# Start addresses of the large SBUF tiles in a four-layer transformer kernel on one core

## Chip, core and metric

The kernel runs on one core of one Trainium2 chip. The metric is the device time of one execution in microseconds (us). Three runs of the kernel before gave 1937.42, 1938.02 and 1940.01 us; their median is 1938.02 us.

## What is computed

The input is one sequence of 512 tokens with 1024 features. It goes through two blocks of two layers each; all weights and activations are float32. The parts that the change touches are these:

```python
# block 1, layer 0: RG-LRU mixer; layer 1: stick-breaking attention; each followed by a SwiGLU
def _rglru_mixer(h, ...):
    proj = h @ w_in                               # gate_br, x_br
    xc = causal depthwise conv of x_br, 4 taps, plus conv_b
    r, i = sigmoid(xc @ w_r + b_r), sigmoid(xc @ w_i + b_i)   # 4 blocks of 256 x 256
    a = exp(8 * r * log_sigmoid(lam)); u = sqrt(1 - a*a) * (i * xc)
    hs = linear scan over time of (a, u)
    return (hs * gelu(gate_br)) @ w_out
def _stick_breaking_attention(q, k, v):           # 16 heads of 64
    z = q k^T / 8
    w[t] = sigmoid(z[t]) * product of sigmoid(-z[s]) over the keys s between t and the query
    return w @ v
# block 2, even layer: global, windowed and memory attention; odd layer: neighbourhood and memory attention
```

Everything else is matrix products with RMS norms, softmax and gates around them.

## The kernel before, in words

**Layout of the work.** Features lie on the 128 partitions, the 512 tokens along the free axis, so that an activation of 1024 features is eight tiles of [128, 512]. A float32 value is split into two parts of the type float32r, a high part `h` and the rest `l`, and a product is three matmuls (`mm3`, lines 161 to 163): high weight times high activation, high weight times low activation, low weight times high activation. The first operand of a matmul is the stationary one (128 columns of a weight tile), the second the moving one (256 or 512 columns of an activation tile).

```python
def mm3(self, out, wh, wl, xh, xl, start, stop):
    mm = self.nc.tensor.matmul
    mm(out, wh, xh, start=start, stop=False)      # L161
    mm(out, wh, xl, start=False, stop=False)      # L162
    mm(out, wl, xh, start=False, stop=stop)       # L163
```

`proj` runs `mm3` over the k-tiles of one output tile, 24 matmuls for 1024 inputs, into one PSUM bank. In `v_proj` (lines 569 to 571) the roles are exchanged: a 128-token piece of an activation tile is stationary and a weight tile moves, the bank changes after every third matmul. The same `mm3` also multiplies two activation tiles: the scores and values of the memory attention. The scores of the global attention are lines 1085 and 1086, its values lines 1118 and 1119; there too both operands are activation tiles. Matmuls that turn a [128, 128] piece (lines 684, 957, 1108, 1186, 1432) have a piece of an `f` tile as the stationary operand and the identity as the moving one.

**Buffers.** All tiles come from one pool with one buffer each; they are laid one behind the other in the order in which they are asked for, each rounded up to 32 bytes per partition. Rings (`Slots`) hand them out oldest-freed first:

| tiles | bytes in a partition | used for | start in the partition, multiples of 2048 taken off |
|---|---|---|---|
| s0-s47, k0-k3 | 32 each | factors per partition | - |
| r0-r59 (float32r) | 2048 each | activations, keys, queries, values, split | 1792 |
| f0-f25 (float32, 516 columns) | 2064, laid 2080 apart | everything not split, residual | all different, multiples of 32 |
| w32 x3, wh x6, wl x6 | 2048 each | weights as loaded, high part, low part | 576 |
| par, ones, mhalf, ebase, lamc, warm, ident, identb, sbmask, fgain, pair | small | constants | - |

The first tile of the pool lies at byte 16512, so r0 is at 18176, wh_0 at 201280 and wl_0 at 213568. A weight tile holds four k-tiles of 128 columns; their stationary operands start 512 bytes apart, at 576, 1088, 1600 and 64 (multiples of 2048 taken off), against 1792 of a moving activation tile.

**Order of the work.** `fetch` (line 134 on) takes the weights in the order of a plan, 512 columns at a time: SP's queue loads a `w` tile, ScalarE writes `wh` (line 142), VectorE writes `wl` (line 143). Up to six chunks are ready ahead. The order on TensorE is the order of tracing: in the attention layers the projections of the next heads are traced between the scores and the values of the present ones, so that TensorE works while VectorE and ScalarE do the softmax.

**Places that the change touches.** In `rglru` the projection is multiplied by the norm into columns 3 to 514 of an `f` tile (line 398), after GpSimd has cleared columns 0 to 2 (line 397); GpSimd starts the convolution (line 401) and three VectorE instructions add the other taps over all 512 columns (line 403), eight times. In `sb_score` (lines 649 to 654) each head's running product is an exclusive scan: GpSimd writes 1.0 into a column, VectorE scans w keys into the w columns behind it, and w of the w + 1 columns are used; 64 times. `warm` (line 105 on) clears its own [128, 512] bfloat16 tile and runs 11 matmuls on it before the first weights are there.

Of the kernel before, what the change touches and what calls it, by code (L numbers as in the profile page):

```python
# [29 lines left out]
FW = 516  # L30


class Slots:
    """Fixed buffers handed out oldest-freed first; the order of tracing gives the waits."""
# [30 lines left out]
class Net:  # L65
    def __init__(self, ctx, tc, nc, a):
# [6 lines left out]
        self.keep = Slots([cp.tile([128, 8], F32, name=f"k{i}") for i in range(4)])  # L73
        self.R = Slots([cp.tile([128, 512], F32R, name=f"r{i}") for i in range(N_R)])
        self.F = Slots([cp.tile([128, FW], F32, name=f"f{i}") for i in range(N_F)])
        self.P = Slots([pp.tile([128, 512], F32, name=f"p{i}") for i in range(8)])
# [3 lines left out]
        self.plan, self.fetched, self.ready = [], 0, deque()  # L80
        self.taken, self.pinned = 0, set()
        par = cp.tile([128, N_PARAM], F32, name="par")
        nc.sync.dma_start(par, a["params"])
        self.par = par
        ones = cp.tile([128, 1], F32, name="ones")
        nc.vector.memset(ones, 1.0)
        self.ones = ones
        mhalf = cp.tile([128, 8], F32, name="mhalf")
        nc.scalar.activation(mhalf, ones.to_broadcast([128, 8]), AF.Copy, scale=-0.5)
        self.mhalf = mhalf  # L90
        ebase = cp.tile([128, 8], F32, name="ebase")
        nc.vector.memset(ebase, 2.718281828459045)
        self.ebase = ebase
        self.scr = cp.tile([128, 32], F32, name="lamc")

    def const(self, name, n):
        t = self.cp.tile([128, n], F32, name=name)
        self.nc.sync.dma_start(t, self.a["c_" + name])
        return t

    def warm(self, n=10):
        """Keeps the tensor engine busy while the first tiles are loaded."""
        nc = self.nc
        z = self.cp.tile([128, 512], BF16, name="warm")
        nc.vector.memset(z, 0.0)
        ps = self.P.get()
        for _ in range(n):
            nc.tensor.matmul(ps, z[:, 0:128], z, start=True, stop=True)
        self.P.put(ps)

# [4 lines left out]
    def small(self, n, keep=False):  # L115
        """Scratch for per-partition scalars; a ring, so short-lived unless `keep`."""
        ring = self.keep if keep else self.sm
        t = ring.get()
        ring.put(t)
        return t[:, 0:n]  # L120
# [6 lines left out]
    def chunks(self, key, width):  # L127
        """Adds the array slice `key` (name, indices...) to the plan, CH columns at a time."""
        for c0 in range(0, width, CH):
            self.plan.append((key, c0, min(width, c0 + CH)))  # L130
# [18 lines left out]
    def weights(self, key, c0=0):  # L149
        """The plan's next chunk as two float32r parts whose sum is the weight."""  # L150
        pinned = min(self.pinned, default=len(self.plan))
        while self.fetched < min(len(self.plan), pinned + N_W) and len(self.ready) <= AHEAD:
            self.fetch()
        self.taken = self.fetched - len(self.ready)
        k, c, h, l = self.ready.popleft()
        assert (k, c) == (key, c0), ((k, c), (key, c0))
        return h, l
# [7 lines left out]
    def open(self, key, kt, off=0, out=None, n=512):  # L165
        """A product over kt k-tiles, run in one or more pieces."""
# [20 lines left out]
    def proj(self, key, XH, XL, off=0, out=None, n=512):  # L187
        """key: [128, K] of weights, k-tile by k-tile; returns a PSUM tile [128, n]."""
        return self.advance(self.open(key, len(XH), off, out, n), XH, XL)

    def split(self, src, eng="v"):
        """float32 [128, 512] in SBUF -> two float32r tiles."""
# [34 lines left out]
    def rstd(self, src, cols, width=D, keep=False):  # L227
        """src: [128, n] sums of squares laid by token -> 1/sqrt(mean + eps)."""
# [12 lines left out]
    def spread(self, r, cols):  # L241
        """r [128 tokens, blocks] -> tile [128, 128 * blocks] with r along the free axis."""
# [12 lines left out]
    def norm_end(self, st, acc, shifted=False):  # L255
        """Factors by token for blocks 0, 128, 256, 384 and, half a block on, 64, 192, 320."""
# [8 lines left out]
    def tok(self, st):  # L265
        """1/rms by token, on partitions."""
# [4 lines left out]
    def row(self, st):  # L271
        """1/rms of every token on every partition."""
# [5 lines left out]
    def residual_norm(self, ms, gain, late=False, shifted=False):  # L278
        """ms: callables that finish residual tile k; splits x * gain and gathers the norm."""
# [25 lines left out]
    def start_out(self, outs, name, kt, YH, YL, tiles=2, last=None):  # L305
        """Runs the first output tiles, kept in `outs`, over the k-tiles at hand (the last one up to `last`)."""
# [32 lines left out]
    def lam_consts(self):  # L339
        """c/2 with c = 8 log_sigmoid(lam), and -c/2."""  # L340
# [43 lines left out]
    def rglru(self, st, gain_next):  # L384
# [5 lines left out]
        for kind, n in self.RG_STEPS:  # L390
            if kind == "x":
                xcs, ch, cl = [], [], []
                for mt in range(2):
                    m = 2 * n + mt
                    ps = self.proj(("w_rg", 8 + m), st["XH"], st["XL"])
                    xbt, xb = self.f(515)
                    pool.memset(xb[:, 0:3], 0.0)
                    v.tensor_tensor(xb[:, 3:515], ps, self.row(st), op=ALU.mult)
                    self.P.put(ps)
                    xct, xc = self.f()  # L400
                    pool.tensor_scalar(xc, xb[:, 3:515], self.p("conv_w", 24 + m), self.p("conv_b", m), op0=ALU.mult, op1=ALU.add)
                    for j in (2, 1, 0):
                        v.scalar_tensor_tensor(xc, xb[:, j : j + 512], self.p("conv_w", 8 * j + m), xc, op0=ALU.mult, op1=ALU.add)
# [70 lines left out]
    def silu_part(self, ps, R):  # L474
        """PSUM gate -> tile A with silu(gate) = A / 2."""
# [40 lines left out]
    def stack_q(self, q32):  # L516
        """[head A; head B] float32 -> [hA; lA] and [hB; lB], each [128, 512] float32r."""
# [11 lines left out]
    def stack_k(self, k32):  # L529
        """[head A; head B] float32 -> per head ([h; h], [l; l]) float32r."""  # L530
# [14 lines left out]
    def v_evac(self, ps, r, out):  # L545
        """PSUM [128 tokens, heads * 64] times r -> out [128, heads * 128] laid [h l] per head."""
# [7 lines left out]
    def v_proj(self, keys, lhs, n):  # L554
        """keys: per k-tile (key, column) of weights [128, n]; lhs(k, t): (h, l) [128, 128] of
        activations for token tile t. Returns a PSUM tile per token tile."""
# [18 lines left out]
    def fold_heads(self, oA, oB):  # L575
        """Two heads' PSUM [from h; from l] -> float32 tile [A; B] of the sums."""
# [10 lines left out]
    def evac_split(self, ps, n):  # L587
        """PSUM [:, :n] -> (h, l) float32r tiles."""
# [37 lines left out]
    def sb_score(self, QK, A, parts):  # L626
        """parts: (head, q-block, column) sharing one bank; keys run backwards from the diagonal."""
# [21 lines left out]
        for idx, (hd, i, o) in enumerate(parts):  # L649
            w = 128 * (i + 1)  # L650
            c = o + idx
            nc.gpsimd.memset(it[:, c : c + 1], 1.0)
            nc.vector.tensor_tensor_scan(it[:, c + 1 : c + 1 + w], a[:, o : o + w], self.zeros[:, :w], 1.0, op0=ALU.mult, op1=ALU.add)  # L653
            nc.vector.tensor_tensor(wt[:, o : o + w], b[:, o : o + w][:, ::-1], it[:, c : c + w][:, ::-1], op=ALU.mult)
# [13 lines left out]
    def sb_values(self, W, V, between):  # L668
        """Weights [query, key] and values -> the pair's output, split."""
# [4 lines left out]
        def turn(*blocks):  # L674
            """blocks: (head, query blocks, key block), one after the other."""
# [54 lines left out]
    def sb_mixer(self, st, gain_next):  # L730
        nc, cp = self.nc, self.cp
        self.identb = cp.tile([128, 128], BF16, name="identb")
# [3 lines left out]
        self.sbmask = cp.tile([128, 256], BF16, name="sbmask")  # L736
# [57 lines left out]
    def double_norm(self, ms):  # L794
        """x <- rmsnorm(x, final_g), and the split of x * final_g * gain2[0] for the next layer."""
        nc = self.nc
        fg = self.p("final_g", 0, 8)
        gain = self.cp.tile([128, 8], F32, name="fgain")
# [40 lines left out]
    def mem_kv(self, layer):  # L839
        """Keys [dim, 256] of two heads per tile and values [token, 512], all split."""  # L840
# [139 lines left out]
    def gated(self, yt, A):  # L980
        """(A / 2) * y, split."""
# [35 lines left out]
    def rope(self, ps, R, g, gs):  # L1017
        """Rotated q * g (before its own rms) and a callable for the rms factors [128 tokens, 2 * block + head]."""
# [80 lines left out]
    def gqa_value(self, W, V):  # L1099
        """Turn and product steps; V[j]: [128 keys, 128] = [h | l] of the head's values."""  # L1100
# [40 lines left out]
    def win_score(self, Q, K, hd):  # L1141
        """hd: head number; softmax with sink over the keys WIN[b] of query block b."""
# [60 lines left out]
    def pair_values(self, value, W, V, between, after=None):  # L1203
        """Both heads of a pair; `between` is issued while the turned weights are split, `after` while the result is."""
# [15 lines left out]
    def even_mixer(self, st, gain_next):  # L1220
# [10 lines left out]
        self.pairsel = self.const("pair", 2)  # L1231
# [144 lines left out]
    def grid_bias(self):  # L1376
        """rpb_c as bias[head][query (col, row) of 16 columns][key (col, row) of 32 columns]."""
# [9 lines left out]
    def na_score(self, Q, K, hd):  # L1387
# [15 lines left out]
        # (query block, first key, keys, bias, place)  # L1403
# [173 lines left out]
    def final(self, name, YH, YL, outs):  # L1577
        """Residual and last norm; the last two tiles run half by half so that the first half's output overlaps."""
# [45 lines left out]
    def run(self, stop=None):  # L1624
# [9 lines left out]
        self.ident = self.const("ident", 128)  # L1634
# [21 lines left out]
def _cols(w, m0=0, m1=None):  # L1656
    """[K, M] -> [M/128, 128, K]: per 128 columns, the k-tiles side by side."""
# [5 lines left out]
def _rows(w):  # L1663
    """[K, n] -> [128, K/128 * n]: the k-tiles side by side."""
# [8 lines left out]
def _arrays(i):  # L1673
# [30 lines left out]
    g4 = np.stack([i["a_w_r"][0], i["a_w_i"][0]], 1)  # [4, 2, 256, 256]  # L1704
# [73 lines left out]
def _grid_order():  # L1778
    """Token number (row-major on the grid) at each place of the column-major order."""
# [33 lines left out]
```

## Time and profile before

| | |
|---|---|
| median of three runs | 1938.02 us (1937.42 to 1940.01) |
| span of the profiled execution, first to last instruction | 1936.2 us; its time as a run is not listed apart, so the span stands 1.8 us below the median |
| TensorE busy (matmuls / weight loads) | 1893.0 us, 98% / 1546.1 us, 80% |
| VectorE, ScalarE, GpSimd busy | 62%, 46%, 17% |
| DMA | 204 MB, 37% of 16 engines |
| granted TensorE clock, mean over the span | 0.997 of 2.4 GHz |

How to read it: a matmul's record runs from its start to the modelled end of its output, some 0.39 us, and the next one starts long before that; records overlap. So TensorE's busy time says only where it had no gap, and what a matmul costs is the distance from its start to the next one's start. The timeline shows starts to 0.01 us; a distance is taken over many matmuls.

### The profile page before, as it was taken

How to read it: one execution, taken by the hardware profiler on the slowest of the kernel's cores; microseconds unless marked ns; L12 is line 12 of the kernel's file. 1: busy time of each engine (PE TensorE's matmuls, PEld its weight loads, DVE VectorE, ACT ScalarE, POOL GpSimd, SP SyncE). 2: the span in 40 equal slices, each digit the busy share in tenths (PEclk: the TensorE clock that was granted, in tenths of full speed). 3: DMA queues.
4: the chain of work that ended last, by engine and by line, in shares of the span. 5: the costliest groups of instructions: out<-in, count | busy, mean ns of one | idle time of the engine just before them, and what ended most of it. 6: DMA issues, size and time to landing. Idle time of an engine off the chain costs nothing. (4 is left out here: it accounts for less than half of the span.)

```text
span 1936.2 us, 25837 instructions
## 1 busy us (share of the span) xinstructions
PE 1893.0 (98%) x9003; PEld 1546.1 (80%) x9003; DVE 1208.5 (62%) x2181; ACT 881.8 (46%) x1701; POOL 330.9 (17%) x386
## 2 busy tenths in 40 slices
PE   8999999999999999999999999999999999999998
PEld 5778888888888777788888888888878888888877
DVE  8886555553336888555555336679897665776753
ACT  4764333333335565433333335456565444455542
POOL 5442000000001211200000121222212421322310
PEclk9999999999999999999999999999999999999999
DMA  4333333333334443333333334322433432554532
GB/s 137 113 106 104 92 96 95 93 93 94 95 96 134 135 124 99 93 92 93 94 95 103 101 109 132 98 77 60 111 106 96 120 104 87 141 146 137 141 99 73
DMA packets 124803, 204.04 MB, mean 105 GB/s; under 512 B 21209, under 2 KB 31193, under 8 KB 124673
## 3 DMA queue, kind: packets, MB, share of 16 engines
q1 hardware_dynamic: 124672, 202.39, 37.4%
q8 instruction: 71, 1.16, 0.3%
q14 instruction: 60, 0.48, 0.1%
HBM read 168.76 MB, written 4.40 MB: 89 GB/s over the span
## 5 line engine op out<-in xcount | busy, mean ns | idle before, releaser
L162 PE MATMUL p<-r,wh 128*128 128x512 f32 (+1 forms) x2216 | 864.5, 390 | 7.1 <-DVE r L223 5.5
L163 PE MATMUL p<-r,wl 128*128 128x512 f32 (+1 forms) x2216 | 864.5, 390 | 6.5 <-DVE wl L143 6.4
L161 PE MATMUL p<-r,wh 128*128 128x512 f32 (+1 forms) x2216 | 868.0, 392 | 0.1
L142 ACT CAST wh<-w 128x512 fp32r<-128x512 f32 x608 | 371.1, 615 | 677.4 <-PE p L162 499.8
L143 DVE TENSOR_TENSOR wl<-w,wh 128x512 fp32r<-128x512 f32 x608 | 443.0, 732 | 352.2 <-ACT wh L142 345.5
L163 PEld LDWEIGHTS p<-r,wl 128*128 128x128 f32 x2216 | 416.8, 188 | 104.2 <-DVE wl L143 9.6
L162 PEld LDWEIGHTS p<-r,wh 128*128 128x128 f32 x2216 | 417.2, 188 | 102.7 <-DVE r L223 7.6
L161 PEld LDWEIGHTS p<-r,wh 128*128 128x128 f32 x2216 | 416.8, 188 | 94.6 <-ACT wh L142 1.7
L198 POOL TENSOR_TENSOR r<-f,r 128x512 fp32r<-128x512 f32 x102 | 141.6, 1390 | 471.5 <-ACT r L196 451.9
L196 ACT CAST r<-f 128x512 fp32r<-128x512 f32 x146 | 90.7, 621 | 176.4 <-DVE f L504 65.5
L214 POOL TENSOR_TENSOR f<-f,f 128x512 f32<-128x512 f32 x40 | 55.4, 1391 | 492.9 <-ACT f L208 492.9
L478 DVE TENSOR_TENSOR f<-p,f 128x512 f32<-128x512 f32 x68 | 47.0, 691 | 89.8 <-PE p L163 89.0
L593 DVE TENSOR_TENSOR r<-p,r 128x512 fp32r<-128x512 f32 (+2 forms) x152 | 90.6, 640 | 4.1 <-ACT r L592 3.6
L592 ACT CAST r<-p 128x512 fp32r<-128x512 f32 (+2 forms) x152 | 77.3, 558 | 12.2 <-PE p L1108 5.7
L569 PE MATMUL p<-wh,r 128*128 128x512 f32 (+1 forms) x192 | 72.1, 375 | 1.0 <-DVE f L582 1.0
L502 DVE TENSOR_TENSOR f<-p,f 128x512 f32<-128x512 f32 x44 | 30.4, 692 | 67.1 <-PE p L163 67.1
L571 PE MATMUL p<-wh,r 128*128 128x512 f32 (+1 forms) x192 | 71.8, 374 | 0.0
L570 PE MATMUL p<-wl,r 128*128 128x512 f32 (+1 forms) x192 | 71.8, 374 | 0.0
L481 ACT ACTIVATE f<-f 128x512 f32<-128x512 f32 x68 | 43.1, 633 | 39.8 <-DVE f L478 39.8
L653 DVE TENSOR_TENSOR_SCAN f<-f,f 128x128 f32<-128x128 f32 (+3 forms) x64 | 51.0, 828 | 14.1 <-ACT f L645 14.1
L921 DVE TENSOR_SCALAR f<-f,s 128x256 f32<-128x256 f32 (+3 forms) x160 | 56.6, 418 | 1.1
L482 DVE SCALAR_TENSOR_TENSOR f<-f,f 128x512 f32<-128x512 f32 x68 | 47.3, 696 | 12.1 <-ACT f L481 7.9
(216 smaller groups left out, 1812.1 us busy)
## 6 DMA issues: line engine op xcount, KB each, us to landing
w<-w_gu SPq DMA_DIRECT2D x176, 256.0 KB, 3.0
r<-r SPq DMA_DIRECT2D x240, 128.0 KB, 2.5
w<-w_d SPq DMA_DIRECT2D x80, 256.0 KB, 2.7
w<-wo_m SPq DMA_DIRECT2D x64, 256.0 KB, 2.9
w<-we_m SPq DMA_DIRECT2D x52, 256.0 KB, 3.0
w<-w_rg SPq DMA_DIRECT2D x32, 256.0 KB, 2.9
w<-w_sqk SPq DMA_DIRECT2D x32, 256.0 KB, 2.9
w<-we_o SPq DMA_DIRECT2D x24, 256.0 KB, 2.6
```

The lines of the kernel that those rows point to most:

```text
L142: nc.scalar.copy(h[:, :n], w[:, :n])
L143: nc.vector.tensor_tensor(l[:, :n], w[:, :n], h[:, :n].bitcast(F32), op=ALU.subtract)
L161: mm(out, wh, xh, start=start, stop=False)
L162: mm(out, wh, xl, start=False, stop=False)
L163: mm(out, wl, xh, start=False, stop=stop)
L196: nc.scalar.copy(h, src)
L198: e.tensor_tensor(l, src, h.bitcast(F32), op=ALU.subtract)
L569: mm(o, xh, h[:, s], start=st, stop=False)
L570: mm(o, xh, l[:, s], start=False, stop=False)
L571: mm(o, xl, h[:, s], start=False, stop=sp)
L592: nc.scalar.copy(h[:, :n], ps[:, :n])
L593: nc.vector.tensor_tensor(l[:, :n], ps[:, :n], h[:, :n].bitcast(F32), op=ALU.subtract)
```

## The change

The large tiles (r, f, w32, wh, wl) become 2048 bytes each and are asked for behind all small ones; a pad of 28 columns (128 bytes as laid) puts the first of them, r0, at byte 20480, ten times 2048. From there each follows the last, so that every large tile starts at a multiple of 2048 (r0 20480, f0 143360, w32_0 196608, wh_0 202752, wl_0 215040). Their numbers stay the same. What lay in the way goes: f tiles have 512 columns instead of 516, the convolution and the scan get along without extra columns, and `warm` borrows an f tile. The rest of the diff takes comments and docstrings out.

```diff
+SMALL_PAD = 28
-FW = 516
+FW = 512
...
         self.keep = Slots([cp.tile([128, 8], F32, name=f"k{i}") for i in range(4)])
+        self.P = Slots([pp.tile([128, 512], F32, name=f"p{i}") for i in range(8)])
...
+        par = cp.tile([128, N_PARAM], F32, name="par")
+        ones = cp.tile([128, 1], F32, name="ones")
...
+        self.ident = cp.tile([128, 128], F32, name="ident")
+        self.identb = cp.tile([128, 128], BF16, name="identb")
+        self.sbmask = cp.tile([128, 256], BF16, name="sbmask")
+        self.fgain = cp.tile([128, 8], F32, name="fgain")
+        self.pairsel = cp.tile([128, 2], F32, name="pair")
+
+        cp.tile([128, SMALL_PAD], F32, name="pad")
         self.R = Slots([cp.tile([128, 512], F32R, name=f"r{i}") for i in range(N_R)])
         self.F = Slots([cp.tile([128, FW], F32, name=f"f{i}") for i in range(N_F)])
...
-        z = self.cp.tile([128, 512], BF16, name="warm")
-        nc.vector.memset(z, 0.0)
+        t, f = self.f(256)
+        z = f.bitcast(BF16)
+        nc.vector.memset(f, 0.0)
         ps = self.P.get()
         for _ in range(n):
             nc.tensor.matmul(ps, z[:, 0:128], z, start=True, stop=True)
         self.P.put(ps)
+        self.F.put(t)
...
-                    xbt, xb = self.f(515)
-                    pool.memset(xb[:, 0:3], 0.0)
-                    v.tensor_tensor(xb[:, 3:515], ps, self.row(st), op=ALU.mult)
+                    xbt, xb = self.f()
+                    v.tensor_tensor(xb, ps, self.row(st), op=ALU.mult)
...
-                    pool.tensor_scalar(xc, xb[:, 3:515], self.p("conv_w", 24 + m), self.p("conv_b", m), op0=ALU.mult, op1=ALU.add)
+                    pool.tensor_scalar(xc, xb, self.p("conv_w", 24 + m), self.p("conv_b", m), op0=ALU.mult, op1=ALU.add)
                     for j in (2, 1, 0):
-                        v.scalar_tensor_tensor(xc, xb[:, j : j + 512], self.p("conv_w", 8 * j + m), xc, op0=ALU.mult, op1=ALU.add)
+                        d = 3 - j
+                        v.scalar_tensor_tensor(xc[:, d:], xb[:, : 512 - d], self.p("conv_w", 8 * j + m), xc[:, d:], op0=ALU.mult, op1=ALU.add)
...
-            c = o + idx
-            nc.gpsimd.memset(it[:, c : c + 1], 1.0)
-            nc.vector.tensor_tensor_scan(it[:, c + 1 : c + 1 + w], a[:, o : o + w], self.zeros[:, :w], 1.0, op0=ALU.mult, op1=ALU.add)
-            nc.vector.tensor_tensor(wt[:, o : o + w], b[:, o : o + w][:, ::-1], it[:, c : c + w][:, ::-1], op=ALU.mult)
+            nc.gpsimd.memset(it[:, o : o + 1], 1.0)
+            nc.vector.tensor_tensor_scan(it[:, o + 1 : o + w], a[:, o : o + w - 1], self.zeros[:, : w - 1], 1.0, op0=ALU.mult, op1=ALU.add)
+            nc.vector.tensor_tensor(wt[:, o : o + w], b[:, o : o + w][:, ::-1], it[:, o : o + w][:, ::-1], op=ALU.mult)
```

## Rows read from the trace of the kernel before

**Rows 1.** The page: span, busy time and instructions of each engine

```profile
span 1936.2 us, 25837 instructions
PE 1893.0 (98%) x9003; PEld 1546.1 (80%) x9003; DVE 1208.5 (62%) x2181; ACT 881.8 (46%) x1701; POOL 330.9 (17%) x386
```

**Rows 2.** Waits of TensorE: engine, line, waited for: us in total, times, longest

```profile
PE p L163 <- DVE wl L143: 6.4, 6, 2.6
PE p L162 <- DVE r L223: 5.5, 5, 3.4
PE p L635 <- DMA r<-r: 4.0, 5, 1.1
```

**Rows 3.** Groups by line and shape: count, busy us and mean ns, idle before

```profile
L161 PE MATMUL p<-r,wh 128*128 128x512 f32 x2104 | 836.4, 398 | 0.1
L569 PE MATMUL p<-wh,r 128*128 128x512 f32 x160 | 63.1, 395 | 1.0 <-DVE f L582 1.0
L161 PE MATMUL p<-r,wh 128*128 128x256 f32 x112 | 31.6, 282 | 0.0
L569 PE MATMUL p<-wh,r 128*128 128x256 f32 x32 | 8.9, 279 | 0.0
L684 PE MATMUL p<-ident,f 128*128 128x128 f32 x160 | 19.2, 273 | 0.4 <-DVE f L654 0.4
```

**Rows 4.** Timeline of TensorE, first SwiGLU: start us, us; first and 48th next

```profile
262.10 0.40 PE L161 MATMUL p<-r,wh 128*128 128x512 f32 x1
...
273.30 0.40 PE L161 MATMUL p<-r,wh 128*128 128x512 f32 x1
```

**Rows 5.** Timeline of TensorE, scores of the global attention; eleven distances

```profile
1299.42 0.39 PE L1086 MATMUL p<-r,r 128*128 128x512 f32 x1
...
1301.91 0.43 PE L161 MATMUL p<-r,wh 128*128 128x512 f32 x1
```

**Rows 6.** Timeline of TensorE, memory attention: values of one head, then scores

```profile
1597.66 0.39 PE L161 MATMUL p<-r,r 128*128 128x512 f32 x1
...
1598.35 0.39 PE L161 MATMUL p<-r,r 128*128 128x512 f32 x1
1598.58 0.39 PE L162 MATMUL p<-r,r 128*128 128x512 f32 x1
1598.80 0.39 PE L163 MATMUL p<-r,r 128*128 128x512 f32 x1
1599.03 0.28 PE L161 MATMUL p<-r,r 128*128 128x256 f32 x1
1599.14 0.28 PE L162 MATMUL p<-r,r 128*128 128x256 f32 x1
...
1600.22 0.28 PE L162 MATMUL p<-r,r 128*128 128x256 f32 x1
```

**Rows 7.** Timeline of TensorE, `v_proj` of the stick-breaking layer; 47 distances

```profile
556.06 0.39 PE L569 MATMUL p<-wh,r 128*128 128x512 f32 x1
...
566.82 0.39 PE L571 MATMUL p<-wh,r 128*128 128x512 f32 x1
```

**Rows 8.** Timeline of TensorE, memory keys, 256 columns, even layer; 27 distances

```profile
1183.89 0.28 PE L161 MATMUL p<-r,wh 128*128 128x256 f32 x1
...
1186.95 0.28 PE L161 MATMUL p<-r,wh 128*128 128x256 f32 x1
```

**Rows 9.** Stretches, line L161 alone: us, PE busy (x), weight loads, clock, DMA

```profile
0.00:190.00 190.00, 93.88 (x235) 44.58 (x235) 0.99 0.39 116
190.00:554.00 364.00, 204.76 (x518) 97.20 (x517) 1.00 0.35 94
554.00:790.00 236.00, 65.84 (x165) 30.93 (x165) 0.99 0.41 113
1230.00:1490.00 260.00, 96.66 (x247) 46.21 (x246) 1.00 0.32 88
```

**Rows 10.** Instructions of single lines on VectorE and GpSimd: duration ns min/median/max

```profile
L397 POOL MEMSET f<- x8: 100/100/101, 0.7 to 60.3; 128x3 f32 x8
L403 DVE SCALAR_TENSOR_TENSOR f<-f,par,f x24: 737/747/1782, 32.9 to 87.8; 128x512 f32<-128x512 f32 x24
```

More of the change, by code (lines that the diff above doesn't have):

```diff
@@ L73, in __init__ @@
         self.keep = Slots([cp.tile([128, 8], F32, name=f"k{i}") for i in range(4)])
+        self.P = Slots([pp.tile([128, 512], F32, name=f"p{i}") for i in range(8)])
+        self.plan, self.fetched, self.ready = [], 0, deque()
+        self.taken, self.pinned = 0, set()
+        par = cp.tile([128, N_PARAM], F32, name="par")
+        ones = cp.tile([128, 1], F32, name="ones")
+        mhalf = cp.tile([128, 8], F32, name="mhalf")
+        ebase = cp.tile([128, 8], F32, name="ebase")
+        self.scr = cp.tile([128, 32], F32, name="lamc")
+        self.ident = cp.tile([128, 128], F32, name="ident")
[4 more added lines that the diff above has]
+        cp.tile([128, SMALL_PAD], F32, name="pad")
         self.R = Slots([cp.tile([128, 512], F32R, name=f"r{i}") for i in range(N_R)])
         self.F = Slots([cp.tile([128, FW], F32, name=f"f{i}") for i in range(N_F)])
-        self.P = Slots([pp.tile([128, 512], F32, name=f"p{i}") for i in range(8)])
         self.w32 = Slots([cp.tile([128, CH], F32, name=f"w32_{i}") for i in range(3)])
@@ L79, in __init__, with const @@
         self.wl = Slots([cp.tile([128, CH], F32R, name=f"wl_{i}") for i in range(N_W)])
-        self.plan, self.fetched, self.ready = [], 0, deque()
-        self.taken, self.pinned = 0, set()
-        par = cp.tile([128, N_PARAM], F32, name="par")
         nc.sync.dma_start(par, a["params"])
         self.par = par
-        ones = cp.tile([128, 1], F32, name="ones")
         nc.vector.memset(ones, 1.0)
         self.ones = ones
-        mhalf = cp.tile([128, 8], F32, name="mhalf")
         nc.scalar.activation(mhalf, ones.to_broadcast([128, 8]), AF.Copy, scale=-0.5)
         self.mhalf = mhalf
-        ebase = cp.tile([128, 8], F32, name="ebase")
         nc.vector.memset(ebase, 2.718281828459045)
         self.ebase = ebase
-        self.scr = cp.tile([128, 32], F32, name="lamc")
-    def const(self, name, n):
-        t = self.cp.tile([128, n], F32, name=name)
+    def const(self, t, name):
         self.nc.sync.dma_start(t, self.a["c_" + name])
-        return t
     def warm(self, n=10):
         nc = self.nc
-        z = self.cp.tile([128, 512], BF16, name="warm")
-        nc.vector.memset(z, 0.0)
+        t, f = self.f(256)
+        z = f.bitcast(BF16)
+        nc.vector.memset(f, 0.0)
         ps = self.P.get()
@@ L648, in sb_score @@
         it, wt = self.F.get(), self.F.get()
-        for idx, (hd, i, o) in enumerate(parts):
+        for hd, i, o in parts:
             w = 128 * (i + 1)
-            c = o + idx
-            nc.gpsimd.memset(it[:, c : c + 1], 1.0)
-            nc.vector.tensor_tensor_scan(it[:, c + 1 : c + 1 + w], a[:, o : o + w], self.zeros[:, :w], 1.0, op0=ALU.mult, op1=ALU.add)
-            nc.vector.tensor_tensor(wt[:, o : o + w], b[:, o : o + w][:, ::-1], it[:, c : c + w][:, ::-1], op=ALU.mult)
+            nc.gpsimd.memset(it[:, o : o + 1], 1.0)
+            nc.vector.tensor_tensor_scan(it[:, o + 1 : o + w], a[:, o : o + w - 1], self.zeros[:, : w - 1], 1.0, op0=ALU.mult, op1=ALU.add)
+            nc.vector.tensor_tensor(wt[:, o : o + w], b[:, o : o + w][:, ::-1], it[:, o : o + w][:, ::-1], op=ALU.mult)
         self.F.put(bt, at, it)
@@ L730, in sb_mixer @@
     def sb_mixer(self, st, gain_next):
-        nc, cp = self.nc, self.cp
-        self.identb = cp.tile([128, 128], BF16, name="identb")
+        nc = self.nc
         nc.gpsimd.tensor_copy(self.identb, self.ident)
@@ L735, in sb_mixer @@
         nc.sync.dma_start(m, self.a["c_sbmask"])
-        self.sbmask = cp.tile([128, 256], BF16, name="sbmask")
         for j in range(2):
@@ L797, in double_norm @@
         fg = self.p("final_g", 0, 8)
-        gain = self.cp.tile([128, 8], F32, name="fgain")
+        gain = self.fgain
         nc.vector.tensor_tensor(gain, fg, self.p("gain2", 0, 8), op=ALU.mult)
@@ L1230, in even_mixer @@
         self.cos, self.sin, self.band = const("c_cos", 512), const("c_sin", 512), const("c_band", 384)
-        self.pairsel = self.const("pair", 2)
+        self.const(self.pairsel, "pair")
         self.window_bias()
@@ L1633, in run @@
         st = self.residual_norm(ms, self.p("mix_g", 0, 8), late=True)
-        self.ident = self.const("ident", 128)
+        self.const(self.ident, "ident")
         st = self.rglru(st, self.p("ffn_g", 0, 8))
```

## The prediction

> **What bounds the kernel now.** I read the page first: TensorE is busy for 98% of the span, every other engine for 62% or less [rows 1]. Then its waits, to see what the missing 2% are: the largest two sum to 12 us, and eighteen more lines, the longest of them 4.0 us, make up the rest [rows 2]. So the time is that of the stream of matmuls, and a change that touches no count and no shape can only matter through the distance from one matmul's start to the next, or through those waits. The groups by shape give the counts [rows 3]: 2104 matmuls of line 161 with 512 columns and as many of lines 162 and 163, so 6312 of the main form (an activation tile moves over a piece of a weight tile); 480 of `v_proj` with 512 columns, 3 x 112 = 336 and 3 x 32 = 96 with 256 columns.
>
> The timeline then gives the distances, and here the trace says something that the busy share hides. In the first SwiGLU 48 distances of the main form take 273.30 - 262.10 = 11.20 us, 233.3 ns each [rows 4]. The scores of the global attention have the same shape and type, but both operands are activation tiles: 11 distances in 2.49 us, 226.4 ns each [rows 5]. The clock is at its upper level, 2.4 GHz, in both places (1.00 granted in the second and the fourth stretch of [rows 9]; the mean over the span is 0.997). The count of accumulated matmuls is no cause either: the memory attention runs the same three lines 161 to 163 into one bank with both operands from activation tiles, and there the distances start near 230 and are 230, 220 and 230 ns at the end, 0.68 us for three, 226.7 each [rows 6]. `v_proj`, where a weight tile moves and an activation tile is stationary, needs 10.76 us for 47 distances, 228.9 each [rows 7].
>
> What tells these forms apart in the program is the start addresses. Activation against activation: both at 1792 plus multiples of 256 bytes, their difference a multiple of 512. Main form: 1792 against 576, 1088, 1600 or 64, the difference always 320 more than a multiple of 512. `v_proj`: moving at 576, a difference of 192 or 448. After the change every large tile starts at a multiple of 2048 and a weight piece at a multiple of 512, so the main form gets the relation that the fast form has now. Whether a tile crosses a multiple of 2048 is not what counts: the memory keys' halves lie alternately across such a place and clear of it, and run 3.06 us for 27 distances without a step, 113.3 each [rows 8].
>
> **The change part by part.**
> - *Main form.* 6312 distances fall from 233.3 to 226.7 ns (the steady value inside [rows 6], a little over that of [rows 5]): 6312 x 6.6 = 41.7 us. This price is not shown for a weight tile, so it needs bounds: nothing, if the weight tiles are slow for another reason; 4.4 ns each (28 us) if they land where `v_proj` is; and a loss of 6.7 ns (42 us) by the rival below. I take the value of the row nearest in form, the same lines with other operands.
> - *v_proj.* 480 x 2.2 = 1.1 us gained, 0 to 3 us.
> - *256 columns.* Here the present relation is the better one: the memory keys run at 113.3 ns [rows 8], activation against activation at 1.08 us for nine, 120.0 [rows 6]. 336 x 6.7 and 96 x up to 2 cost 2.4 us; I take 2, since part of them runs slower than 113 already.
> - *Settling.* The fast form takes about six matmuls after a break to reach 226.7: in [rows 6] the first three take 0.69 us (229 to 230 each, 1597.66 to 1598.35). Some 90 stretches between attention blocks, at most 20 to 30 ns each: 2 us.
> - *What the stalls take back.* A faster stream only makes TensorE arrive earlier where it waits. In the first 190 us the 235 triples would gain 235 x 3 x 6.6 = 4.7 us [rows 9], but its waits on the split of activations and weights by VectorE stand in this stage [rows 2]; I count all of it as lost. In the stick-breaking stage (165 triples, 3.3 us) and the even layer's attention (247, 4.9 us less what is not main form, some 4.3), a wait for the softmax or for a tile's transfer follows most blocks; I count half, 3.8 us. Late next, there, is VectorE. Together 8.5 us, with bounds of 0 and 15. The two SwiGLU stages and the output products have no waits and keep everything.
> - *Convolution.* Eight clears of 100 ns leave GpSimd, and 24 VectorE instructions of 747 ns process 1 to 3 columns of 512 fewer [rows 10], under 5 ns each: 0.8 us and 0.1 us off engines that are busy 17% and 62%. The clear was ready long before; I count nothing. If its cover (the projection on TensorE) were gone, the gain would be 0.1 us per tile. The write of the projection now reaches a ring buffer first, where the clear used to; its readers ended many buffers ago, so no wait moves with it. The taps stay in VectorE's order, no DMA moves, and SP's and GpSimd's queues lose the clears alone.
> - *Scan.* 64 scans shorten by one element, some 2 ns each: nothing. *warm* clears the same 1024 bytes, and its f buffer comes back some 18 buffers later: nothing. *Other addresses* of VectorE's, ScalarE's and the DMA's operands: no row prices them, but TensorE's waits would show it, 12 us in the two largest, and not on weight loads.
>
> Sum: -41.7 - 1.1 + 2 + 2 + 8.5 = -30.3 us on the profiled span of 1936.2 us, so 1905.9; its span stands 1.8 us below the median of the runs, so **1907.7 us**. Its own bounds: with no stall taking anything and the fast value at once, -41, 1897; with 15 us taken, -24, 1914.
>
> **A rule against it.** The rows show a distance that differs between forms with the same shape. The Trainium skill, TensorE: Matmul & The Clock Gate, section "Part 2: What happens when you issue a matmul", says that TensorE has two independent read ports into SBUF, one for the moving operand and one for weight loads, and that loading the next weights takes no bandwidth from the running matmul. By that rule the two addresses could not disturb each other, and the sum would be about zero. The trace agrees that loads run beside matmuls (80% and 98% busy), but not that the form of the operands is without effect.
>
> **Rivals.**
> 1. *The place is not the cause.* Weight tiles may be slow because they lie high in the partition, above byte 196608, or because VectorE and ScalarE write them at the time; then the distance stays 233.3 and only the trifles above remain: 1938 us, within 3. For it: every slow form has a weight operand. Against it: with 256 columns the form with weights is the faster one, 113.3 against 120.0 [rows 6, 8], which a slow region would not give. Chance 0.17.
> 2. *Weights land in between.* The main form settles at the 228.9 of `v_proj` [rows 7]: 6312 x 4.4 = 28 us, less some 11 for the same deductions: 1921 us. Chance 0.11.
> 3. *The equal relation is the worse one for loads from a weight tile.* What the 256-column rows show, 6.7 ns more per matmul when both operands stand in the same relation [rows 6, 8], would then hold for 512 columns: 6312 x 6.7 = 42 us more, 1980 us, fully paid, since TensorE is the bound. It decides in the first projection after 30 us: 240 ns instead of 233. Against it: with 512 columns the same relation is the fast one in two places [rows 5, 6]. Chance 0.10.
>
> **How the numbers follow.** The forecast has 0.62, rival 1 0.17, rival 2 0.11, rival 3 0.10. A change of 0.2%, 3.9 us, is about what a measurement can tell from none. Faster: 0.62 + 0.11 = 0.73; the same: 0.17; slower: 0.10. The forecast's own range is 1890 to 1914: its bounds, and a little below for a distance under 226.7; rival 2 takes it to 1925. These two hold 0.73, so the range has to reach rival 1 as well, to 1940, and leaves rival 3 out: 1890 to 1940.
>
> **What would show it.** Right: in the SwiGLU stages 48 matmuls take 10.88 us instead of 11.20; lines 161 to 163 with 512 columns have means of some 390 ns instead of 398 (the pipeline's end moves with the distance); the memory keys go to 120 ns; the waits on VectorE grow by some us in the attention stages. If the distance stays 233.3, the address is no cause and rival 1 holds; if it is 229, rival 2; if it is 240, rival 3. If the distance falls and the time falls by less than 24 us, the stalls have taken more than I counted.

## The result and the profile after

The changed kernel takes 1907.55 us (median of four runs, 1906.63 to 1908.69) against 1937.72 us for the kernel before in the same session (four runs). The ratio is 0.9844, with a 95% interval of 0.9833 to 0.9856: 30.2 us less. The forecast was 1907.7 us. In the text below, lines 161 to 163 of before are lines 169 to 171 of after, `v_proj` is lines 577 to 579, the split of weights lines 150 and 151, and the split of normed activations on VectorE line 231. Where a run puts a pad line ahead of these, its numbers are one higher.

The page of the profile after, first lines, against [rows 1]. This execution took 1906.63 us as a run, its span stands 2.2 us below that:

```profile
span 1904.4 us, 25828 instructions
...
PE 1859.4 (98%) x9003; PEld 1550.5 (81%) x9003; DVE 1205.3 (63%) x2181; ACT 880.0 (46%) x1701; POOL 328.6 (17%) x378
```

The count of matmuls is the same and so is the share of busy time. TensorE's idle time is 1904.4 - 1859.4 = 45.0 us, where it was 43.2. So the 31.8 us that left the span left it inside the stream of matmuls, and no view that shows only gaps could have told it. GpSimd has lost the eight clears of the convolution (386 to 378 instructions).

The groups by line and shape on TensorE, kernel after, against [rows 3]:

```profile
L169 PE MATMUL p<-r,wh 128*128 128x512 f32 x2104 | 826.6, 393 | 0.1
...
L577 PE MATMUL p<-wh,r 128*128 128x512 f32 x160 | 62.8, 393 | 0.7 <-DVE f L590 0.7
...
L169 PE MATMUL p<-r,wh 128*128 128x256 f32 x112 | 32.2, 287 | 0.0
...
L577 PE MATMUL p<-wh,r 128*128 128x256 f32 x32 | 9.1, 283 | 0.0
```

With 512 columns a record became shorter (398 to 393 and 395 to 393 ns), with 256 columns longer (282 to 287 and 279 to 283). The records overlap, so these means give only the sign; the size is in the timeline. The prediction had named some 390 ns for 512 columns.

The timeline of TensorE, kernel after, first SwiGLU (start us, us; the first and the 51st next matmul), against [rows 4]:

```profile
261.77 0.39 PE L169 MATMUL p<-r,wh 128*128 128x512 f32 x1
...
273.33 0.39 PE L169 MATMUL p<-r,wh 128*128 128x512 f32 x1
```

51 distances in 11.56 us are 226.7 ns each, where 48 took 11.20 us, 233.3 each. The timeline of `v_proj` after, first and 96th matmul, against [rows 7]:

```profile
543.29 0.39 PE L577 MATMUL p<-wh,r 128*128 128x512 f32 x1
...
564.83 0.39 PE L579 MATMUL p<-wh,r 128*128 128x512 f32 x1
```

95 distances in 21.54 us: also 226.7. And the memory keys with 256 columns after, 27 distances, against [rows 8]:

```profile
1158.85 0.28 PE L169 MATMUL p<-r,wh 128*128 128x256 f32 x1
...
1162.09 0.28 PE L169 MATMUL p<-r,wh 128*128 128x256 f32 x1
```

3.24 us, 120.0 ns each, where it was 113.3.

**Where the time came from.** I added up, over both traces, the distance from each matmul's start to the next one's, by form:

| form | count | total before, us | total after, us | steady distance before and after, ns |
|---|---|---|---|---|
| main form, 512 columns | 6312 | 1503.5 | 1469.0 | 233.3, 227.0 |
| `v_proj`, 512 columns | 480 | 112.2 | 110.6 | 230.0, 227.3 |
| main form, 256 columns | 336 | 39.8 | 41.4 | 115.0, 119.8 |
| `v_proj`, 256 columns | 96 | 11.3 | 11.5 | 117.8, 120.0 |
| activation with activation, and all others | 1779 | 261.1 | 263.7 | |

The steady distance is the mean of those without a wait or a lower clock in them (245 ns and less with 512 columns, 130 and less with 256). The sum is -34.5 - 1.6 + 1.6 + 0.2 + 2.6 = -31.7 us, and the span lost 31.8. The fast distance alone would have brought 6312 x 6.3 = 39.8 us in the main form; 5 us of that were given back.

**What gave it back.** The waits of TensorE, kernel after, against [rows 2]:

```profile
PE p L171 <- DVE wl L151: 7.1, 7, 2.7
PE p L170 <- DVE r L231: 5.5, 5, 3.5
PE p L643 <- DMA r<-r: 4.3, 5, 0.9
PE p L642 <- DMA r<-r: 2.9, 4, 1.8
```

They hardly grew: all waits of this view sum to 37.7 us, against 35.6 before, and those on VectorE went from 21.9 to 21.5. What grew are the waits on transfers, from 9.4 to 11.8 us. In this execution more went to the clock. The stretches of TensorE, here first the kernel after (us, PE busy and instructions, granted clock, DMA share, GB/s):

```profile
0.00:30.00 30.00, 22.28 (x75) 0.89 0.60 176
30.00:190.00 160.00, 153.49 (x663) 0.98 0.35 104
```

and the kernel before, the same stretches:

```profile
0.00:30.00 30.00, 22.62 (x80) 0.94 0.62 176
30.00:190.00 160.00, 153.62 (x660) 1.00 0.35 104
```

By 190 us both have started the same number of matmuls, 738 and 740, although each costs over 6 ns less. The lower mean clock is worth 0.05 x 30 + 0.02 x 160 = 4.7 us, as much as the first stage had to gain. The timeline of TensorE, kernel after, shows one of the places:

```profile
83.07 0.50 PE L171 MATMUL p<-r,wl 128*128 128x512 f32 x1 [2.19 <-DVE wl L151]
83.41 0.41 PE L169 MATMUL p<-r,wh 128*128 128x512 f32 x1
83.64 0.61 PE L170 MATMUL p<-r,wh 128*128 128x512 f32 x1
84.04 0.63 PE L171 MATMUL p<-r,wl 128*128 128x512 f32 x1
84.47 0.63 PE L169 MATMUL p<-r,wh 128*128 128x512 f32 x1
...
87.28 0.39 PE L170 MATMUL p<-r,wh 128*128 128x512 f32 x1
```

After a wait of 2.19 us the starts are 0.43 us apart instead of 0.23, and the records 0.63 us long, for some 3.4 us: TensorE runs at the lower of its two levels, 1.2 GHz (granted clock 0.50 from 83.7 to 87.0 us). The same follows a wait of 3.45 us (lower level from 16.6 to 22 us) and one of 2.68 us (121.3 to 124.6). In these 190 us the kernel before has it once, from 17.1 to 19.9 us. Such a wait is not always followed by it; the timeline of TensorE, kernel before, after a wait of 2.64 us:

```profile
120.27 0.50 PE L163 MATMUL p<-r,wl 128*128 128x512 f32 x1 [2.64 <-DVE wl L143]
120.60 0.40 PE L161 MATMUL p<-r,wh 128*128 128x512 f32 x1
120.84 0.40 PE L162 MATMUL p<-r,wh 128*128 128x512 f32 x1
```

There the granted clock from 121.4 to 124.5 us is 1.00. Between 190 and 1899 us each kernel has one more stretch at 0.50, before from 757 to 761 us and after from 1811 to 1814 us, both behind waits of only some 1.5 us.

### The profile page after: what moved, and what is told of

Read it like the earlier page. It is cut to its first block, busy times and chain, and to the rows that moved or that the text cites. A ratio compares the mean times of both kernels' runs of the same rounds, so it can differ in the third digit from the quotient of the medians.

```text
span 1904.4 us, 25828 instructions
## 1 busy us (share of the span) xinstructions
PE 1859.4 (98%) x9003; PEld 1550.5 (81%) x9003; DVE 1205.3 (63%) x2181; ACT 880.0 (46%) x1701; POOL 328.6 (17%) x378
## 5 line engine op out<-in xcount | busy, mean ns | idle before, releaser
L171 PE MATMUL p<-r,wl 128*128 128x512 f32 (+1 forms) x2216 | 855.8, 386 | 7.1 <-DVE wl L151 7.1
L170 PE MATMUL p<-r,wh 128*128 128x512 f32 (+1 forms) x2216 | 855.2, 386 | 7.1 <-DVE r L231 5.5
L169 PE MATMUL p<-r,wh 128*128 128x512 f32 (+1 forms) x2216 | 858.8, 388 | 0.1
L171 PEld LDWEIGHTS p<-r,wl 128*128 128x128 f32 x2216 | 418.3, 189 | 92.4 <-DVE wl L151 10.3
L660 DVE TENSOR_TENSOR_SCAN f<-f,f 128x127 f32<-128x127 f32 (+3 forms) x64 | 50.6, 822 | 14.2 <-ACT f L653 14.2
```

## The experiments

The theory: a matmul's distance is set by the difference between the start addresses of its stationary and its moving operand, and by nothing else of the change. The rivals: the absolute place in the partition, or a multiple of 2048 for its own sake, is what counts; or the time comes from the convolution, the scan and the f tiles' length. Most edits move only the tiles of the weights, by a pad tile ahead of them; the activations stay. What each run left is shown by the timeline of TensorE in the first SwiGLU: the first and the last record between 262.0 and 273.4 us, a row of one form without a break. The table behind the experiments puts the distances together.

**Pad alone, in the kernel before.** The weight tiles move by 192 bytes, from 576 to 768 (multiples of 2048 taken off), so that their difference to 1792 is a multiple of 256. Nothing else of the change is in it: the f tiles keep 516 columns, no large tile begins at a multiple of 2048.

```diff
 self.P = Slots([pp.tile([128, 512], F32, name=f"p{i}") for i in range(8)])
+cp.tile([128, 48], F32, name="shift")
 self.w32 = Slots([cp.tile([128, CH], F32, name=f"w32_{i}") for i in range(3)])
```

> The kernel before with 192 bytes of pad ahead of the weight tiles and nothing else: weight pieces start at 768, 1280, 1792 and 256 (multiples of 2048 taken off) against 1792 of the activations, so the difference of stationary and moving start becomes a multiple of 512, while no large tile lies at a multiple of 2048 and the padded rows stay. If the relation of the two addresses is the cause: 226.7 ns between the matmuls of the main form, 120 ns with 256 columns, 1905 to 1911 us, as the whole change. If multiples of 2048 themselves are needed, or the cause lies in the f tiles, the convolution or the scan: 233.3 ns and 1935 to 1941 us.

Measured: 1907.33 us, ratio 0.9849 (0.9833 to 0.9866). Its timeline, 51 distances, 226.7 ns:

```profile
261.71 0.39 PE L163 MATMUL p<-r,wh 128*128 128x512 f32 x1
...
273.27 0.39 PE L163 MATMUL p<-r,wh 128*128 128x512 f32 x1
```

One line does what the whole diff does. The weight tiles still lie above byte 201000, and ScalarE and VectorE still write them at the time, so neither the height in the partition nor the writing made them slow.

**Convolution and scan alone, in the kernel before.** The lines of the diff from `xbt, xb` on; the f tiles keep their 516 columns, so that no address moves.

```diff
-                    xbt, xb = self.f(515)
-                    pool.memset(xb[:, 0:3], 0.0)
-                    v.tensor_tensor(xb[:, 3:515], ps, self.row(st), op=ALU.mult)
+                    xbt, xb = self.f()
+                    v.tensor_tensor(xb, ps, self.row(st), op=ALU.mult)
...
-            nc.vector.tensor_tensor_scan(it[:, c + 1 : c + 1 + w], a[:, o : o + w], self.zeros[:, :w], 1.0, op0=ALU.mult, op1=ALU.add)
+            nc.vector.tensor_tensor_scan(it[:, o + 1 : o + w], a[:, o : o + w - 1], self.zeros[:, : w - 1], 1.0, op0=ALU.mult, op1=ALU.add)
```

> The other part alone: convolution and scan without the extra columns, on the layout of before (f tiles still 516 columns long). By the theory of addresses nothing on TensorE changes: 233.3 ns, 1934 to 1941 us, the same as before within 0.2%. If the new convolution and scan brought a part of the gain, the time falls below 1934 us and the waits of TensorE on VectorE in the first 190 us shrink.

Measured: 1937.86 us, ratio 1.0 (0.999 to 1.0009), ten runs. GpSimd's instructions are 378, as in the changed kernel, so the edit is in it. Its timeline, 49 distances in 11.44 us, 233.5 ns:

```profile
261.80 0.40 PE L162 MATMUL p<-r,wh 128*128 128x512 f32 x1
...
273.24 0.39 PE L163 MATMUL p<-r,wl 128*128 128x512 f32 x1
```

This part of the change is worth nothing. It was needed only to make room.

**The changed kernel with the old difference.** 64 bytes ahead of the weight tiles; everything else stays changed, and the activations stay at multiples of 2048.

```diff
 self.F = Slots([cp.tile([128, FW], F32, name=f"f{i}") for i in range(N_F)])
+cp.tile([128, 16], F32, name="shift")
 self.w32 = Slots([cp.tile([128, CH], F32, name=f"w32_{i}") for i in range(3)])
```

> The kernel after with 64 bytes of pad ahead of the weight tiles: activations stay at multiples of 2048, weight pieces start 64 above a multiple of 512. If the addresses are the cause, the main form falls back to 230 to 233.3 ns, the 256-column form to 113 to 118, and the time to 1930 to 1940 us. If 64 bytes do not matter (a coarser relation, or the f tiles' place): 226.7 ns and 1905 to 1911 us.

Measured: 1937.76 us, ratio 1.0003 (0.9992 to 1.0014). 49 distances in 11.44 us:

```profile
261.76 0.40 PE L170 MATMUL p<-r,wh 128*128 128x512 f32 x1
...
273.20 0.39 PE L171 MATMUL p<-r,wh 128*128 128x512 f32 x1
```

64 bytes take the whole gain back.

**All large tiles 64 bytes off a multiple of 2048.** The differences stay as in the changed kernel, the places do not.

```diff
-SMALL_PAD = 28
+SMALL_PAD = 44
```

> The kernel after with a pad 64 bytes longer ahead of all large tiles: every large tile starts 64 above a multiple of 2048, the difference of stationary and moving start stays a multiple of 512. If only the difference of the two addresses counts: 226.7 ns, 1905 to 1911 us. If each operand has to be aligned by itself (the moving one, the stationary one, or both, to 128 bytes or more): 228.9 to 233.3 ns and 1920 to 1940 us.

Measured: 1910.34 us (1908.36 to 1912.58), ratio 0.9862 (0.9847 to 0.9877). 51 distances in 11.56 us, 226.7 ns:

```profile
261.66 0.39 PE L170 MATMUL p<-r,wh 128*128 128x512 f32 x1
...
273.22 0.39 PE L170 MATMUL p<-r,wh 128*128 128x512 f32 x1
```

The multiple of 2048 plays no part; the tiles may all lie across it. The 2.8 us to the changed kernel are not in the distance, and they are hardly shown: the intervals of the two ratios overlap (0.9847 to 0.9877 and 0.9833 to 0.9856). The mean granted clock does not settle them either: the profiled execution has 0.991 over its span and 0.77 in its first 30 us, and is the fastest of the four runs.

**The period.** The changed kernel with 256 bytes ahead of the weight tiles asks whether 256 or 512 bytes is the period.

```diff
+cp.tile([128, 64], F32, name="shift")
```

> The kernel after with 256 bytes of pad ahead of the weight tiles. If the relation repeats every 128 or 256 bytes: 226.7 ns and 1905 to 1911 us. If only every 512: up to 233.3 ns and 1938 us.

Measured: 1910.03 us (two runs), ratio 0.9852 (0.9809 to 0.9896). 51 distances in 11.56 us:

```profile
261.81 0.39 PE L171 MATMUL p<-r,wh 128*128 128x512 f32 x1
...
273.37 0.39 PE L171 MATMUL p<-r,wh 128*128 128x512 f32 x1
```

A difference of 256 is as good as one of 0.

**Half a period, and an eighth.** 128 and 32 bytes ahead of the weight tiles.

```diff
+cp.tile([128, 32], F32, name="shift")
```

> The kernel after with 128 bytes of pad ahead of the weight tiles. If the relation repeats every 128 bytes: 226.7 ns and 1905 to 1911 us, as the kernel after. If it repeats every 256 or 512 bytes: slower than 226.7, up to 233.3 ns and 1938 us.

```diff
+cp.tile([128, 8], F32, name="shift")
```

> The kernel after with 32 bytes of pad ahead of the weight tiles: the difference of stationary and moving start is 32 above a multiple of 512. If any difference that is no multiple of 128 disturbs: 230 to 233.3 ns, 1925 to 1940 us. If what counts is a step of 32 bytes: 226.7 ns, 1905 to 1911 us. A value apart from both, say 280 or 272 clock steps replaced by another, would be new.

Measured: 1936.76 us for 128, ratio 0.9993 (0.9982 to 1.0005), and 1940.01 us for 32, ratio 1.001 (0.9999 to 1.0022). The timeline with 128 bytes, 50 distances, 232.4 ns:

```profile
261.63 0.39 PE L170 MATMUL p<-r,wh 128*128 128x512 f32 x1
...
273.25 0.39 PE L172 MATMUL p<-r,wl 128*128 128x512 f32 x1
```

Neither is fast: not every power of two helps, and 32 bytes are already too much. The 280 and 272 steps of the expectation are 233.3 and 226.7 ns counted at 1.2 GHz; at 2.4 GHz, the level of these stretches, they would be 560 and 544.

**One of three matmuls disturbed.** The 64 bytes stand between the `wh` and the `wl` tiles, so that only line 172, which multiplies the low weights, has the old difference.

```diff
 self.wh = Slots([cp.tile([128, CH], F32R, name=f"wh_{i}") for i in range(N_W)])
+cp.tile([128, 16], F32, name="shift")
 self.wl = Slots([cp.tile([128, CH], F32R, name=f"wl_{i}") for i in range(N_W)])
```

> The kernel after with 64 bytes of pad between the high and the low weight tiles: two of the three matmuls of a triple keep a difference that is a multiple of 512, the third has one of 64 more. If each matmul pays by its own operands: the triple takes 2 x 226.7 + 233.3 = 687 ns, a third of the gain is lost, 1914 to 1920 us. If one disturbed matmul throws the next ones out of step (a settled stream needs about six): 700 ns for the triple, 1930 to 1938 us.

Measured: 1929.5 us (1927.33 to 1932.54), ratio 0.9951 (0.9937 to 0.9964). The timeline, 50 distances in 11.55 us, 231.0 ns; in the middle, two lines 172 and what lies between them:

```profile
261.75 0.39 PE L170 MATMUL p<-r,wh 128*128 128x512 f32 x1
...
269.14 0.40 PE L172 MATMUL p<-r,wl 128*128 128x512 f32 x1
269.37 0.39 PE L170 MATMUL p<-r,wh 128*128 128x512 f32 x1
269.60 0.39 PE L171 MATMUL p<-r,wh 128*128 128x512 f32 x1
269.83 0.40 PE L172 MATMUL p<-r,wl 128*128 128x512 f32 x1
...
273.30 0.40 PE L172 MATMUL p<-r,wl 128*128 128x512 f32 x1
```

Three matmuls take 693 ns. Were each to pay for its own difference alone, it would be 2 x 226.7 + 233.3 = 687; were one enough to put all three out of step, 700. It is neither. One slow matmul costs its neighbours something: their distances in the whole stretch are 228 and 229 ns, its own up to the next start is 236. How the time of a triple divides among its lines says little by itself: with 160 bytes (below), where all three have the same difference, lines 170 to 172 have steady means of 231.9, 233.2 and 234.9 ns over the whole trace. The `w32` and `wh` tiles stay in place here, so it is the address of an operand of TensorE that acts, not that of the weights as loaded. What exactly waits, the reading of the weights or of the moving operand, this run does not tell, and it stays open.

**The value of `v_proj` in the main form.** 192 bytes ahead of the weight tiles: the main form then has the difference that `v_proj` had in the kernel before (192), and `v_proj`, where the operands change places, has 64.

```diff
+cp.tile([128, 48], F32, name="shift")
```

> The kernel after with 192 bytes of pad ahead of the weight tiles: the main form gets the difference that v_proj had before (192 above a multiple of 256), v_proj the one that the main form had (64). If the difference alone sets the distance, they exchange values: 228.9 ns for the main form, 233.3 for v_proj, about 1920 us. If the form of the work (which operand is the weight, how often the bank changes) sets which of the two slower values comes: 233.3 for the main form, 1938 us.

Measured in one run: 1919.84 us, beside 1940.66 of the kernel before. The timeline of the first SwiGLU, 50 distances in 11.45 us, 229.0 ns:

```profile
261.81 0.39 PE L170 MATMUL p<-r,wh 128*128 128x512 f32 x1
...
273.26 0.39 PE L172 MATMUL p<-r,wl 128*128 128x512 f32 x1
```

and that of `v_proj`, same kernel, 95 distances in 22.16 us, 233.3 ns:

```profile
546.10 0.39 PE L578 MATMUL p<-wh,r 128*128 128x512 f32 x1
...
568.26 0.39 PE L580 MATMUL p<-wh,r 128*128 128x512 f32 x1
```

The two forms have exchanged their values, 233.3 and some 229. Which tile is stationary is no cause; the difference, with its sign, is.

**The rest of the period.** 96, 160 and 224 bytes ahead of the weight tiles, one run each beside the same 1940.66 us.

```diff
+cp.tile([128, 24], F32, name="shift")
```

> The kernel after with 96 bytes of pad ahead of the weight tiles. If only the multiple of 256 is fast: 228.9 to 233.3 ns, 1918 to 1940 us; below 226.7 would show a better place.

```diff
+cp.tile([128, 40], F32, name="shift")
```

> The kernel after with 160 bytes of pad ahead of the weight tiles. If only the multiple of 256 is fast: 228.9 to 233.3 ns, 1918 to 1940 us; below 226.7 would show a better place.

```diff
+cp.tile([128, 56], F32, name="shift")
```

> The kernel after with 224 bytes of pad ahead of the weight tiles, 32 below a multiple of 256. If only the multiple of 256 is fast: 228.9 to 233.3 ns, 1918 to 1940 us. A distance below 226.7 would show that the multiple of 256 is not the best place.

Measured: 1944.28, 1940.46 and 1938.76 us. None is fast; 96 is the slowest of all. Its timeline, 50 distances in 11.71 us, 234.2 ns:

```profile
261.68 0.40 PE L172 MATMUL p<-r,wl 128*128 128x512 f32 x1
...
273.39 0.40 PE L171 MATMUL p<-r,wh 128*128 128x512 f32 x1
```

All runs together; the difference is the start of the stationary operand less that of the moving one, multiples of 256 taken off, in the main form (in `v_proj` it is 256 less this):

| difference, bytes | kernels | 512 columns, ns | 256 columns, ns | time, us |
|---|---|---|---|---|
| 0 | changed; pad alone; all tiles 64 off; 256 bytes | 226.7 | 119.8 | 1907.3 to 1910.3 |
| 32 | 32 bytes | 233.3 | 118.3 | 1940.01 |
| 64 | before; convolution and scan alone; 64 bytes | 233.3 | 115.0 to 115.8 | 1937.7 to 1937.9 |
| 96 | 96 bytes | 234.2 | 118.3 | 1944.28 |
| 128 | 128 bytes | 232.4 | 119.3 | 1936.76 |
| 160 | 160 bytes | 233.3 | 119.9 | 1940.46 |
| 192 | 192 bytes | 228.9 | 117.8 | 1919.84 |
| 224 | 224 bytes | 233.3 | 117.3 | 1938.76 |

The distances with 256 columns are means over those of 130 ns and less, 329 of the 336 of the form. `v_proj` bears the table out from the other side: with 96 bytes, where its own difference is 160, it runs at 233.4 ns, and with 160 bytes, where it is 96, at 234.2, as the main form does at these differences.

## Why the prediction was right

**The main form.** The step said that the fast distance belongs to a relation of start addresses, seen before only between two activation tiles [rows 5, 6], and that weight tiles would reach it. They did, to the value taken, 226.7 ns. The pad alone and the 64 bytes show the cause from both sides: put in where it was missing, it brings all; taken away from the changed kernel, nothing is left. The relation was described too narrowly as one to multiples of 512; it is one to 256.

**Rival 1**, the place: fell with the pad alone, which leaves the tiles where rival 1 blames them. **Rival 2**, 229 ns for weight tiles: fell, but its value was no property of `v_proj`. It is what a difference of 192 gives, in either form, and at 1919.84 us its price of 1921 was right too. **Rival 3**, the equal relation being worse for weights: fell with 512 columns. With 256 it is right: 0 is among the worst differences there.

**The rule against it.** With the pad alone, which moves the tiles of the weights and the small ones behind them, the distance falls by 6.6 ns in the first SwiGLU; with all large tiles moved alike by 64 bytes it stays at 226.7. The two operands' addresses therefore do bear on each other, which the two independent read ports of the Trainium skill, TensorE: Matmul & The Clock Gate, "Part 2: What happens when you issue a matmul", would not give; the measurement decides. That the loads run beside the matmuls stays true (81% and 98% busy).

**256 columns.** Plus 2 us was taken, 1.6 + 0.2 measured, with the 120 ns that was named. **`v_proj`**: 1.1 us predicted, 1.6 measured; it lands at 226.7 (steady mean 227.3). **Settling**: 2 us predicted; the steady mean of 227.0 stands 0.3 ns over 226.7, times 6312 some 2 us.

**What the stalls take back**: 8.5 us was taken; by the steady values the sum without it is -39.8 - 1.3 + 1.8 = -39.3 us (`v_proj` 480 x 2.7 = 1.3), the span lost 31.8, so 7.5 us were taken back. The size was nearly right and so was the place of its first part: the first stage kept nothing of its 4.7 us. But the mechanism was not what the step said. "Late next, there, is VectorE" is wrong: TensorE's waits on VectorE went from 21.9 to 21.5 us, and they did not grow in the attention stages (from 190 us on 9.6 us before, 8.7 after). In the profiled execution 4.7 us by the windows went to the lower clock in the first 190 us, and some 2 us to longer waits on transfers (from 190 us on 9.4 to 11.8 us).

Of these two, only the waits on transfers go with the distance. Summed over the view of waits, one execution of each kernel, they are 11.5 to 12.7 us in the four kernels at 226.7 ns, 10.9 and 10.5 us with 192 bytes and with the `wl` tiles moved, and 8.1 to 10.3 us in the eight kernels at 232 ns and more. That the lower clock is a consequence of the faster matmuls is not shown: with the 64 bytes, where the distance is the old one, the clock is 0.89 in the first 30 us and 0.98 from 30 to 190 us, as in the changed kernel, and with the pad alone, where it is the new one, 0.94 and 0.99. So it is luck in part that 7.5 us stand against 8.5.

**The total.** That the median comes within 0.2 us of the forecast is luck too. On the spans -31.8 us stands against -30.3, the profiled execution is the fastest of its four runs, and a run's time stands 2.2 us above its span where the forecast had 1.8.

**Convolution, scan, `warm`**: nothing was taken, nothing was measured (1.0, 0.999 to 1.0009, for the first two; `warm` was not run alone, but the pad alone has none of it and is as fast).

## What to carry to other kernels

Where TensorE is busy all the time, read the distance from start to start by form of operands, not the busy share: some 6 ns hidden in each of 6312 matmuls brought 1.6% of the time. For matmuls of float32r operands with 512 columns, as here, give the stationary and the moving operand start addresses whose difference is a multiple of 256 bytes; one pad tile can do it, and moving every tile to round addresses adds nothing to that. With 256 columns this difference is not the best, so measure the form that holds most of the work.

## What the runs showed of the hardware that was not expected

- The distance depends on the difference of two addresses, not on either: 226.7 ns at 0 and 256 bytes, 228.9 at 192, 232.4 to 234.2 at 32, 64, 96, 128, 160 and 224. It is not monotonous, and it has a sign: 64 costs 233.3 and 192, its opposite, 228.9.
- With 256 columns the order is another: 115.0 ns at 64 and 119.8 at 0 in the main form, and 113.5 in `v_proj` with a difference of 64 (the 192-byte kernel). Tiles of 512 columns at one difference and of 256 at another were not tried; by the table it would be worth at most 336 x 5 ns, 1.7 us.
- One matmul in three at a difference of 64 cost 693 - 680 = 13 ns per triple, twice what it costs by itself (6.6), so neighbours are slowed too.
- After waits of 2.2 to 3.5 us TensorE of the changed kernel ran for 3 to 6 us at the lower clock level, 0.43 us from start to start; after one of 2.64 us in the kernel before it did not. The windows of the first 30 us show 0.94 (pad alone), 0.89 (changed kernel) and 0.77 (all tiles 64 off) of full clock at one and the same distance. (0.94 - 0.77) x 30 = 5 us is an estimate, from these windows, of the most that they can differ by through the clock of the start.
